# Dilated attention for a prompt: three dilation patterns in sequence, or two pairs of blocks each in turn

## The chip, the core and the metric

The kernel runs on one core of one Trainium2 chip. The metric is the device time of one execution in microseconds (us). The core has TensorE (PE in the profile, with its weight loads as PEld), VectorE (DVE), ScalarE (ACT), GpSimd (POOL) and SyncE (SP, which issues most DMAs here). The profile also gives the clock that TensorE was granted in each stretch, as a share of full speed.

## The reference

One layer of a hybrid decoder trunk, for a prompt of 2048 tokens and a small group of samples. The prompt's attention is the part that matters here:

```python
DIL_PATTERNS = ((128, 1), (512, 4), (2048, 16))     # window, dilation; 8 heads of 64 dims
def _dilated_branch_prompt(q, k, v, dilation, slopes):
    # the tokens of one residue mod `dilation`, in blocks of 128 queries;
    # a block of queries sees its own block of keys and the one before it
    scores = jnp.einsum('bnqchd,bnkchd->bnchqk', qb, kb).astype(jnp.float32) * (HEAD_DIM ** -0.5)
    scores = jnp.where(valid, scores + bias, NEG)
    m = jnp.max(scores, axis=-1, keepdims=True)
    p = jnp.exp(scores - m)
    l = jnp.sum(p, axis=-1, keepdims=True)
    out = jnp.einsum('bnchqk,bnkchd->bnqchd', (p / l).astype(v.dtype), vb)
    lse = m + jnp.log(l)
# the three patterns' outputs are merged with weights softmax(lse)
```

Before it stand the norm and the projection to q, k, v and a pooling input; behind it the output projection and a feed-forward network with a causal convolution, which is most of the time.

## The kernel before

The program has three parts: projections, attention, and output projection with the feed-forward network. Scores and projections use the type float32r (values split into a high and a low part), transposes and products with values use float32.

Attention works on *items*. Each of the 8 heads has three patterns p = 0, 1, 2 (dilation 1, 4, 16), each pattern 16 blocks of 128 queries, and an item is a pair of blocks: 8 items a pattern, 24 a head, 192 in all. A block with a predecessor has 256 keys, one without has 128. Of pattern 0 that is one block in 16 with 128 keys, of pattern 1 four, of pattern 2 all 16: its score matmuls are half as wide, and it has half the transposes and value products. An item is numbered by its place in the list `items` (item 48 is the first of head 2).

An item passes three steps. `scores` (L288, L289): for each block two matmuls (high and low keys) into the PSUM tile `Sp`, of which there are 4; DVE adds the bias table, takes the minimum (L291) and ACT the exponential into `Pt` (L293; 3 buffers). `turn`, two items later: PE transposes (L301), DVE or ACT copies to `PTs` (L304, L306). `values`, three items later: PE multiplies with the values `V` into `Op` (L322; the profile shows two instructions for each such matmul), ACT copies to `O` (L326), and a finished half of a pattern is stored to DRAM (`store_o`).

For patterns 1 and 2 the queries of a head are first copied by POOL into the order of the blocks (`spread_q`, L242: 1024 columns, two buffers). Queries and keys of the next head come in six DMAs of 512 KB (`load_head`, tile `QK`, two buffers) in the third item of a head. Values are held for two heads at a time, 1 MB per pattern in three buffers (`next_v`); those of pattern 2 are loaded in an even head, behind that head's `QK` loads, those of patterns 0 and 1 in the odd head before. All of these go through SP's queue in one order, with the stores between them.

The kernel's framework schedules instructions at build time: each engine gets a fixed list, which is not the order of the source. By its own estimate of when a load lands it lets an engine's later work go ahead of work that would wait. At run time each engine takes its list in order.

The order of the items is this line, and each item calls `advance`:

```python
items = [(h, p, pr) for h in range(H) for p in ((0, 1, 2) if h < H - 1 else (2, 1, 0)) for pr in range(8)]
```

Of the kernel before, what the change touches and what calls it, by code (L numbers as in the profile page):

```python
# [17 lines left out]
P = 128  # L18
# [29 lines left out]
def kernel(ctx, tc, ins, cst, outs):  # L48
# [131 lines left out]
    def load_v(hp, p, t, blocks=slice(0, 16)):  # L180
        vs = v_s[:, hp * P:(hp + 1) * P]
        d = t[:, :, 1:P + 1]
        if p == 0:
            nc.sync.dma_start(d[:, blocks], vs.rearrange("(n i) f -> i n f", i=P)[:, blocks])
        else:
            r, n = DILS[p], S // (P * DILS[p])
            for J in range(n):
                src = vs[J * P * r:(J + 1) * P * r].rearrange("(m c i) f -> i m c f", c=r, i=RUN)
                for i in range(RUN):
                    nc.sync.dma_start(d[i::RUN, r * J:r * (J + 1), :], src[i])  # L190
# [27 lines left out]

    def store_o(p, hp, O, half):
        eng = nc.gpsimd if hp == 3 and p == 0 and half else nc.sync  # L220
        dst = o_s[p * S:(p + 1) * S, hp, :]
        s = slice(8 * half, 8 * half + 8)
        if p == 0:
            eng.dma_start(dst.rearrange("(n i) f -> i n f", i=P)[:, s], O[:, s])
        elif p == 1:
            for J in (2 * half, 2 * half + 1):
                eng.dma_start(dst[J * CH:(J + 1) * CH].rearrange("(i c) f -> i c f", c=4),
                                  O[:, 4 * J:4 * J + 4, :])
        else:
            eng.dma_start(dst.rearrange("(i c) f -> i c f", c=16)[:, s], O[:, s])  # L230

    def spread_q(h, p, half):

        qs = spread[h, p, half] = p2.tile([P, S // 2], F32R, tag="qs", name="qs", bufs=2)
        q, r = heads[h][0], DILS[p]
        if p == 1:
            src = q[:, half * (S // 2):(half + 1) * (S // 2)].rearrange("p (b j c) -> p b c j", b=2, c=r)
            dst = qs.rearrange("p (b c j) -> p b c j", b=2, c=r)
        else:
            src = q.rearrange("p (j c) -> p c j", c=r)[:, half * r // 2:(half + 1) * r // 2]  # L240
            dst = qs.rearrange("p (c j) -> p c j", j=P)
        nc.gpsimd.tensor_copy(dst, src)  # L242
# [8 lines left out]
    def next_v(hp, p):  # L251
        pair_v[hp, p] = value_tile(p2, "V")
        load_v(hp, p, pair_v[hp, p])
# [1016 lines left out]
```

## Time and profile before

| | |
|---|---|
| median of 3 runs | 2542.49 us (2539.44 to 2546.87) |
| the profiled execution | 2538.81 us, its span 2537.0 us |
| mean granted TensorE clock | 0.985 of full speed |
| attention, first score matmul to last value product | 444.8 to 792.9 us of the span |
| busy share of PE, DVE, ACT, POOL | 98%, 68%, 43%, 7% |

Matmuls are pipelined and their ends are modelled, so PE's busy share says little; more is read from how many instructions it gets through in a stretch (the xcount of a row), from the granted clock beside it, and from the waits in brackets in the list of instructions.

### The profile page before, as it was taken

Reading aid. Unit: us, or ns where it says so; the run is one execution under the profiler, and the core shown is the slowest. Engines: PE = TensorE matmul, PEld = TensorE weight load, DVE = VectorE, ACT = ScalarE, POOL = GpSimd, SP = SyncE. Lnnn points to the kernel's source line nnn. Section 1 sums busy time; section 2 is a strip of 40 time slices with the busy share of each in tenths; the row PEclk is TensorE's granted clock in tenths of the full one; section 3 lists DMA queues with packets and bytes.
Section 4 is the critical chain, followed back from the end, with each engine's and each line's share of the span. In section 5 each row is a group of like instructions: output and inputs, shape, how many; then the busy total and the mean of one; then the engine's idle time right before and its main releaser. Section 6 shows DMA issues by size and latency. Waiting matters only on the chain.

```text
span 2537.0 us, 36098 instructions
## 1 busy us (share of the span) xinstructions
PE 2497.4 (98%) x13310; PEld 2126.6 (84%) x13310; DVE 1729.4 (68%) x3819; ACT 1085.1 (43%) x2021; POOL 180.7 (7%) x192
## 2 busy tenths in 40 slices
PE   7999999999998999999999999999999999999999
PEld 5888887899997887888888888888888889999997
DVE  6445445566566775988887788887887666566655
ACT  6333332566564222544443454443443444444442
POOL 1111111222222000000000000000000000000000
PEclk9999999899889999999999999999999999999999
DMA  6343434876655898755558334447443446222321
GB/s 223 102 128 103 129 98 122 197 187 167 143 136 200 286 302 256 238 183 173 182 167 267 100 119 135 145 143 237 145 134 107 125 133 208 87 82 85 93 77 62
DMA packets 412573, 393.60 MB, mean 155 GB/s; under 512 B 16043, under 2 KB 319239, under 8 KB 409708
## 3 DMA queue, kind: packets, MB, share of 16 engines
q1 hardware_dynamic: 412172, 390.48, 50.6%
q8 instruction: 105, 1.72, 0.3%
q0 software_dynamic: 224, 0.80, 0.1%
q14 instruction: 72, 0.59, 0.1%
HBM read 305.70 MB, written 85.52 MB: 154 GB/s over the span
## 4 chain that ended last, share of the span: by engine, by line
PE 94%; DMA 2%; DVE 2%; issue 1%; ACT 0%; POOL 0%; SPq 0%; DVEq 0%; ACTq 0%; POOLq 0%
PE pu L1014 39%; PE pd L1190 19%; PE ps L454 13%; PE po L793 6%; PE Op L322 5%; PE tp L301 3%; PE Sp L288 3%; PE Sp L289 2%; PE tp L122 1%; PE tp L463 1%; PE pd L1184 1%; DVE T L291 0%; PE pp L535 0%; DMA QK<-kT_lo 0%; DMA g_b<-in_g_q_dram 0%
## 5 line engine op out<-in xcount | busy, mean ns | idle before, releaser
L1014 PE MATMUL pu<-h,w 128*128 128x512 f32 (+1 forms) x5232 | 989.0, 349 | 2.2 <-ACT w L112 1.7
L1014 PEld LDWEIGHTS pu<-h,w 128*128 128x128 f32 x5232 | 850.0, 188 | 133.0 <-ACT w L112 2.1
L1190 PE MATMUL pd<-w,act 128*128 128x512 f32 x2112 | 490.2, 392 | 0.0
L1190 PEld LDWEIGHTS pd<-w,act 128*128 128x128 f32 x2112 | 396.7, 188 | 88.0
L112 ACT CAST w<-raw 128x1024 fp32r<-128x1024 f32 (+1 forms) x282 | 286.9, 1026 | 295.4 <-PE pd L1190 187.7
L113 DVE TENSOR_TENSOR w<-raw,w 128x1024 fp32r<-128x1024 f32 (+1 forms) x278 | 329.1, 1187 | 24.3 <-ACT w L112 24.2
L454 PE MATMUL ps<-W_hi,xh 128*128 128x512 f32 x1024 | 332.7, 398 | 1.0 <-ACT xh L112 1.0
L1158 DVE SCALAR_TENSOR_TENSOR cv<-ex,cw,cv 128x512 f32<-128x512 f32 x352 | 262.5, 746 | 29.3 <-ACT cv L1150 26.8
L1148 ACT COPY ex<-pu 128x512 f32<-128x512 f32 (+1 forms) x220 | 110.2, 501 | 341.3 <-PE pu L1014 341.1
L454 PEld LDWEIGHTS ps<-W_hi,xh 128*128 128x128 f32 x1024 | 192.8, 189 | 43.1 <-ACT xh L112 1.5
L291 DVE CUSTOM_DVE_ANT_0 T<-Sp,tab 128x256 f32<-128x256 f32 (+1 forms) x384 | 129.4, 364 | 121.5 <-PE Sp L289 75.9
L293 ACT ACTIVATE Pt<-T,st 128x256 f32<-128x256 f32 (+1 forms) x384 | 162.7, 459 | 97.6 <-DVE st L291 84.1
L454 PE MATMUL ps<-W_lo,xh 128*128 128x512 f32 x512 | 202.8, 396 | 0.0
L1192 DVE TENSOR_TENSOR ya<-ya,pd 128x512 f32<-128x512 f32 x192 | 131.2, 685 | 103.0 <-PE pd L1190 102.4
L95 POOL TENSOR_TENSOR rs<-ms,mhalf 128x8 f32<-128x8 f32 (+3 forms) x68 | 76.4, 1124 | 1584.2 <-DVE stT L1151 1047.7
L322 PE MATMUL Op<-V,PTs 128*128 128x65 f32 x1200 | 174.7, 281 | 0.7 <-DVE PTs L304 0.6
L322 PEld LDWEIGHTS Op<-V,PTs 128*128 128x128 f32 x1200 | 167.2, 207 | 1.7 <-DVE PTs L304 0.8
L1150 ACT ACTIVATE cv<-pu,cw 128x512 f32<-128x512 f32 (+3 forms) x264 | 166.0, 649 | 0.0
L301 PE MATMUL tp<-ident,Pt 128*128 128x128 f32 x600 | 124.4, 294 | 0.1
L112 ACT CAST act<-cv 128x512 fp32r<-128x512 f32 x88 | 54.6, 621 | 159.9 <-DVE cv L1167 153.3
L454 PEld LDWEIGHTS ps<-W_lo,xh 128*128 128x128 f32 x512 | 96.9, 189 | 19.8
L1151 DVE COPY stT<-ex 128x2 f32<-128x2 f32 x176 | 28.9, 164 | 117.7 <-ACT ex L1148 117.5
(225 smaller groups left out, 2759.0 us busy)
## 6 DMA issues: line engine op xcount, KB each, us to landing
raw<-in_w_up_dram SPq DMA_DIRECT2D x176, 512.0 KB
raw<-in_w_down_dram SPq DMA_DIRECT2D x80, 512.0 KB
hn_s<-w SPq DMA_DIRECT2D x16, 1024.0 KB
h<-hn_s SPq DMA_DIRECT2D x32, 512.0 KB
far<-in_cache_k_dram SPq DMA_DIRECT2D x64, 256.0 KB
far<-in_cache_v_dram SPq DMA_DIRECT2D x64, 256.0 KB
om<-o_s SPq DMA_DIRECT2D x16, 792.0 KB
raw<-in_w_in_dram SPq DMA_DIRECT2D x16, 512.0 KB
```

The source lines that it names most:

```text
L112: nc.scalar.copy(hi, src)
L113: (eng or nc.vector).tensor_tensor(out=lo, in0=src, in1=f32(hi), op=ALU.subtract)
L293: nc.scalar.activation(Pt[:, s, :w], T[:, :w], AF.Exp, bias=st[:, i8:i8 + 1], scale=-1.0)
L301: nc.tensor.transpose(tp[:, j, :], Pt[:, s, n * P:(n + 1) * P], ident)
L322: nc.tensor.matmul(Op[:, i4, :], PT[:, j, :], pair_v[hp, p][:, b, v0:v0 + DH + 1], start=n == 0, stop=n == m - 1)
L454: nc.tensor.matmul(ps, xh[:, a, k, :], (W_hi, W_lo)[b][j, k // 2][:, k % 2, :], start=n == 0, stop=n == 3 * KT - 1)
L793: nc.tensor.matmul(ps, lhs, wo[half][k + 4 * (1 - part)][b], start=part == 0 and k == 0 and i == 0, stop=part == 1 and k == 3 and i == 2)
L1014: nc.tensor.matmul(ps[:, :n], w[:, a, k, :], hs[k][:, b, c0:c0 + n], start=i == 0, stop=i == 3 * KT - 1)
L1150: nc.scalar.activation(d, s, AF.Identity, bias=cw[:, 3, ct:ct + 1], scale=cw[:, 2, ct:ct + 1])
L1158: nc.vector.scalar_tensor_tensor(out=d, in0=e[j], scalar=cw[:, j, ct:ct + 1], in1=d, op0=ALU.mult, op1=ALU.add)
L1190: nc.tensor.matmul(ps, act[0][:, a, k, tau * P:(tau + 1) * P], wd[k][:, b, :], start=k == 0 and j == 0, stop=k == n - 1 and j == 2)
L1192: nc.vector.tensor_tensor(out=ysl, in0=ysl, in1=ps, op=ALU.add)
```

## The change

The order of the items becomes one of turns. A turn is two items (four blocks) of one pattern; a head of 1 to 6 takes pattern 0, 2, 1, 0, 2, 1 and so on, four turns each. Head 0 begins with the eight items of pattern 0 as before, head 7 has an order of its own. To go with it, values come in halves of a pattern (8 blocks, six buffers), outputs too, and the copied queries in quarters (512 columns, four buffers, issued six items ahead instead of three). The running minimum `st` and the PSUM tile `Op` are kept per pattern. The first halves of the values of a pair of heads are loaded in the odd head before, all second halves in the even head, behind the loads of `QK`.

```diff
-        t = pool.tile([P, 16, P + 2], F32, tag=tag, name="V", bufs=3 if tag == "V" else 1)
+        t = pool.tile([P, 8 if tag == "V" else 16, P + 2], F32, tag=tag, name="V", bufs=6 if tag == "V" else 1)
...
-    def spread_q(h, p, half):
-
-        qs = spread[h, p, half] = p2.tile([P, S // 2], F32R, tag="qs", name="qs", bufs=2)
+    def spread_q(h, p, k):
+
+        qs = spread[h, p, k] = p2.tile([P, CH], F32R, tag="qs", name="qs", bufs=4)
...
-    def next_v(hp, p):
-        pair_v[hp, p] = value_tile(p2, "V")
-        load_v(hp, p, pair_v[hp, p])
+    def next_v(hp, p, half):
+        t = value_tile(p2, "V")
+        load_v(hp, p, t, 8 * half, 8 * half + 8)
+        for b in range(8):
+            pair_v[hp, p, 8 * half + b] = t[:, b, :]
...
-    items = [(h, p, pr) for h in range(H) for p in ((0, 1, 2) if h < H - 1 else (2, 1, 0)) for pr in range(8)]
+    def turns(seq):
+        at = {}
+        for p in seq:
+            n = at[p] = at.get(p, -1) + 1
+            yield from ((p, 2 * n), (p, 2 * n + 1))
+
+    ORDER = [(0, 0, 0, 0) + (2, 1) * 4] + [(0, 2, 1) * 4] * (H - 2) + [(0, 2, 2, 1, 2, 0, 2, 1, 0, 1, 1, 0)]
+    items = [(h, p, pr) for h in range(H) for p, pr in turns(ORDER[h])]
+    NI = 24
     AHEAD = 8
+    SPREAD = 6
...
-        next_v(0, 1)
-        next_v(0, 2)
+        for half in range(2):
+            for p in (2, 1):
+                next_v(0, p, half)
...
-                h, p, pr = items[i]
-                if (i == AHEAD or h and p == 0 and pr == 3) and h + 1 < H:
+                h, li = divmod(i, NI)
+                if (i == AHEAD or h and li == 4) and h + 1 < H:
                     load_head(h + 1)
-                if h % 2 == 1 and h + 1 < H and p > 0 and pr == 4:
-                    next_v((h + 1) // 2, p - 1)
-                if h % 2 == 0 and h and p == 0 and pr == 4:
-                    next_v(h // 2, 2)
+                for k, p in enumerate((2, 0, 1)):
+                    if h % 2 == 1 and h + 1 < H and li == (14, 17, 21)[k]:
+                        next_v((h + 1) // 2, p, 0)
+                    if h % 2 == 0 and h and li == 4 + k:
+                        next_v(h // 2, p, 1)
```

What the scheduler makes of it shows at the end of head 2. PE before, where `Sp` 5699 to 5809 are items 68 to 73, `qs` marks patterns 1 and 2, and `V_5293` is pattern 2's values: score matmuls of 20 in a row (here the last ten), and then the value products of item 64 and the transposes of item 66.

```order
L289 MATMUL Sp_5745<-QK_4654,qs_5628 128x128
L288 MATMUL Sp_5766<-QK_4654,qs_5628 128x128
L289 MATMUL Sp_5766<-QK_4654,qs_5628 128x128
L288 MATMUL Sp_5789<-QK_5260 128x128
L288 MATMUL Sp_5725<-QK_4654,qs_5628 128x128
L289 MATMUL Sp_5725<-QK_4654,qs_5628 128x128
L288 MATMUL Sp_5809<-QK_5260 128x256
L288 MATMUL Sp_5745<-QK_4654,qs_5628 128x128
L289 MATMUL Sp_5745<-QK_4654,qs_5628 128x128
L289 MATMUL Sp_5789<-QK_5260 128x128
L289 MATMUL Sp_5809<-QK_5260 128x256
L322 MATMUL Op_5695<-V_5293,PTs_5669 128x65 x2
```

PE now at the same place, where `Sp` 5686 to 5814 are items 66 to 71 and `V_5327`, `V_5359`, `V_5387` are the second halves of the values of patterns 2, 0 and 1 (lines have moved: L289 and L290 are the scores, L302 the transposes, L324 the value products).

```order
L290 MATMUL Sp_5686<-QK_4704 128x256
L289 MATMUL Sp_5791<-QK_4704,qs_5640 128x256
L290 MATMUL Sp_5791<-QK_4704,qs_5640 128x256
L289 MATMUL Sp_5708<-QK_4704 128x256
L290 MATMUL Sp_5708<-QK_4704 128x256
L289 MATMUL Sp_5814<-QK_4704,qs_5640 128x256
L290 MATMUL Sp_5814<-QK_4704,qs_5640 128x256
L289 MATMUL Sp_5735<-QK_4704,qs_5585 128x128
L290 MATMUL Sp_5735<-QK_4704,qs_5585 128x128
L324 MATMUL Op_5683<-V_5327,PTs_5658 128x65 x2
L302 MATMUL tp2_5698<-ident_63,Pt_5644 128x128 x4
L324 MATMUL Op_5683<-V_5327,PTs_5680 128x65
```

The run of score matmuls without a transpose or value product is still there, now 19 long, 13 of them 256 wide; before it was 20, of which 2 are 256 wide. What follows it now, up to the next scores of item 72, is this:

```order
L324 MATMUL Op_5633<-V_5359,PTs_5605 128x65 x3
L324 MATMUL Op_5633<-V_5359,PTs_5630 128x65 x4
L324 MATMUL Op_5683<-V_5327,PTs_5680 128x65
L302 MATMUL tp2_5720<-ident_63,Pt_5666 128x128 x4
L324 MATMUL Op_5728<-V_5130,PTs_5703 128x65
L302 MATMUL tp2_5747<-ident_63,Pt_5687 128x128 x4
L289 MATMUL Sp_5765<-QK_4704,qs_5585 128x128
L290 MATMUL Sp_5765<-QK_4704,qs_5585 128x128
L324 MATMUL Op_5728<-V_5387,PTs_5703 128x65
L324 MATMUL Op_5728<-V_5130,PTs_5703 128x65
```

With the rows around them that is 12 transposes, 19 value products (38 instructions in a profile) and two score matmuls. Heads 4 and 6 have such a run at the same place in both kernels, head 0 a shorter one. On SP's queue in head 2, the loads of the next head's `QK` stand ahead of the second halves of the values:

```order
L231 DMA o_s_80<-O_4554 512x1x132 x2
L161 DMA QK_5318<-qT_hi_71 64x2048
L162 DMA QK_5318<-qT_lo_72 64x2048
L165 DMA QK_5318<-kT_hi_73 64x2048
L166 DMA QK_5318<-kT_lo_74 64x2048
L165 DMA QK_5318<-kT_hi_73 64x2048
L166 DMA QK_5318<-kT_lo_74 64x2048
L193 DMA V_5327<-v_s_75 32x8x128 x4
L185 DMA V_5359<-v_s_75 128x8x128
L193 DMA V_5387<-v_s_75 32x4x128 x8
```

Before, the store ahead of them was one DMA (`O_4503`), and behind them stood only the four DMAs of pattern 2's values, of 256 KB each.

## Rows read from the trace of the kernel before

**Rows 1.** The page: busy time by engine, and the clock in 40 slices.
```profile
PE 2497.4 (98%) x13310; PEld 2126.6 (84%) x13310; DVE 1729.4 (68%) x3819; ACT 1085.1 (43%) x2021; POOL 180.7 (7%) x192
...
PEclk9999999899889999999999999999999999999999
```

**Rows 2.** Stretches by head, counting L293's exponentials: length, ACT busy, clock, DMA.
```profile
495.30:532.80 37.50, 20.48 (x48) 1.00 0.72 170
532.80:574.70 41.90, 20.32 (x49) 0.94 0.77 194
...
746.20:790.90 44.70, 20.01 (x48) 0.80 0.24 73
```

**Rows 3.** Stretches with all engines: PE, PEld, DVE, ACT, POOL, clock, DMA, GB/s.
```profile
484.30:491.20 6.90, 5.81 (x29) 5.47 (x29) 2.53 (x15) 2.43 (x7) 0.00 (x0) 0.51 0.53 109
569.70:579.90 10.20, 10.20 (x52) 10.04 (x52) 4.02 (x19) 4.66 (x13) 4.30 (x3) 0.50 0.52 116
651.60:665.20 13.60, 13.37 (x65) 13.22 (x66) 4.19 (x21) 4.91 (x13) 4.26 (x3) 0.50 0.39 85
736.90:764.20 27.30, 27.23 (x133) 26.31 (x134) 13.99 (x64) 13.70 (x40) 7.24 (x6) 0.50 0.21 68
579.90:590.10 10.20, 10.20 (x93) 9.92 (x92) 7.06 (x29) 7.15 (x17) 0.20 (x1) 1.00 0.99 205
487.70:491.10 3.40, 3.40 (x20) 3.40 (x18) 1.45 (x7) 2.03 (x6) 0.00 (x0) 0.50 0.12 29
491.20:494.60 3.40, 3.40 (x30) 3.20 (x30) 1.38 (x5) 1.82 (x5) 2.35 (x3) 1.00 0.51 130
```

**Rows 4.** PE's instructions at the end of head 2, with waits.
```profile
564.71 0.33 PE L288 MATMUL Sp<-QK,qs 128*128 128x128 f32 x1 [0.20 <-DVE st L291]
...
565.87 0.33 PE L288 MATMUL Sp<-QK,qs 128*128 128x128 f32 x1 [0.28 <-DVE st L291]
...
566.82 0.33 PE L288 MATMUL Sp<-QK 128*128 128x128 f32 x1 [0.17 <-DVE st L291]
...
567.98 0.39 PE L288 MATMUL Sp<-QK 128*128 128x256 f32 x1 [0.50 <-DVE st L291]
...
568.75 0.55 PE L322 MATMUL Op<-V,PTs 128*128 128x65 f32 x4
```

**Rows 5.** PE's waits, 455 to 790 us: total, times, longest.
```profile
PE Sp L288 <- DVE st L291: 6.9, 21, 0.7
```

**Rows 6.** DVE by form, 447 to 792 us: busy, mean ns, idle before.
```profile
L291 DVE CUSTOM_DVE_ANT_0 T<-Sp,tab 128x256 f32<-128x256 f32 x216 | 85.2, 422 | 70.4 <-PE Sp L289 44.8 <-ACT O L326 13.0 <-PE tp L301 7.5
...
L291 DVE CUSTOM_DVE_ANT_0 T<-Sp,tab 128x128 f32<-128x128 f32 x168 | 45.4, 290 | 51.1 <-PE Sp L289 31.2 <-PE tp L301 12.1 <-ACT Pt L293 5.8
L291 DVE DVE_READ_ACCUMULATOR2_ANT st<- 128x1 f32 x384 | 31.9, 83 | 0.0
L304 DVE COPY PTs<-tp 128x256 f32<-128x256 f32 x56 | 23.6, 421 | 11.6 <-PE tp L301 11.4
```

**Rows 7.** PE's instructions at the end of head 0, behind its run.
```profile
486.71 1.05 PE L322 MATMUL Op<-V,PTs 128*128 128x65 f32 x4
487.56 0.63 PE L301 MATMUL tp<-ident,Pt 128*128 128x128 f32 x2
...
491.31 0.31 PE L288 MATMUL Sp<-QK,qs 128*128 128x128 f32 x1
```

**Rows 8.** SP's queue in heads 1 and 2: start, time, what it issues.
```profile
526.81 10.27 SPq L190 DMA_DIRECT2D V<-v_s  x16
...
540.24 0.53 SPq L161 DMA_DIRECT2D QK<-qT_hi  x1
```

**Rows 9.** Stretches of DMA in heads 1 and 2, columns as in rows 3.
```profile
541.00:561.00 20.00, 19.97 (x173) 19.31 (x172) 13.78 (x58) 13.43 (x33) 4.39 (x5) 1.00 1.04 230
526.80:537.10 10.30, 10.30 (x89) 10.06 (x89) 6.71 (x37) 7.29 (x22) 6.75 (x7) 1.00 0.43 115
```

**Rows 10.** POOL's instructions as attention begins.
```profile
458.38 2.02 POOL L242 CAST qs<-QK 128x1024 fp32r<-128x1024 f32 x1 [1.20 <-DMA QK<-qT_lo]
```

More of the change, by code (lines that the diff above doesn't have):

```diff
@@ L178, in value_tile, with load_v @@
         return t
-    def load_v(hp, p, t, blocks=slice(0, 16)):
+    def load_v(hp, p, t, lo, hi):
         vs = v_s[:, hp * P:(hp + 1) * P]
@@ L313, in values @@
         st, Pt, blocks = res
-        if h2 == 0 and pr == 0 and h + p:
-            pair_o[p] = p2.tile([P, 16, OW], F32, tag="O", name="O", bufs=3)
-        O = pair_o[p]
+        half, pr4 = divmod(pr, 4)
+        if h2 == 0 and pr4 == 0 and (p, half) not in pair_o:
+            pair_o[p, half] = p2.tile([P, 8, OW], F32, tag="O", name="O", bufs=6)
+        O = pair_o[p, half]
         if pr % 2 == 0:
-            state["Op"] = psum.tile([P, 4, DH + 1], F32, tag="tp", name="Op", bufs=4)
-        Op = state["Op"]
+            state["Op", p] = psum.tile([P, 4, DH + 1], F32, tag="tp", name="Op", bufs=4)
+        Op = state["Op", p]
         v0 = h2 * (DH + 1)
         for j, (s, i4, n, b, m) in enumerate(blocks):
-            nc.tensor.matmul(Op[:, i4, :], PT[:, j, :], pair_v[hp, p][:, b, v0:v0 + DH + 1],
+            nc.tensor.matmul(Op[:, i4, :], PT[:, j, :], pair_v[hp, p, b][:, v0:v0 + DH + 1],
                              start=n == 0, stop=n == m - 1)
@@ L325, in values, with spread_next @@
         if pr % 2:
-            nc.scalar.copy(O[:, 2 * pr - 2:2 * pr + 2, o0:o0 + DH + 1], Op)
-        if pr % 4 == 3:
-            nc.gpsimd.tensor_copy(O[:, 2 * pr - 6:2 * pr + 2, o0 + DH + 1], st)
-        if h2 == 1 and pr % 4 == 3:
-            store_o(p, hp, O, pr // 4)
-    items = [(h, p, pr) for h in range(H) for p in ((0, 1, 2) if h < H - 1 else (2, 1, 0)) for pr in range(8)]
+            nc.scalar.copy(O[:, 2 * pr4 - 2:2 * pr4 + 2, o0:o0 + DH + 1], Op)
+        if pr4 == 3:
+            nc.gpsimd.tensor_copy(O[:, :, o0 + DH + 1], st)
+            if h2 == 1:
+                store_o(p, hp, O, half)
+                del pair_o[p, half]
+    def turns(seq):
[6 more added lines that the diff above has]
+    NI = 24
     AHEAD = 8
+    SPREAD = 6
     attn, PTs = {}, {}
-    SPREAD = 3
+    def spread_next(i):
+        if i < len(items):
+            h, p, pr = items[i]
+            if p and pr % 2 == 0:
+                spread_q(h, p, pr // 2)
     def advance(i):
-        if i + SPREAD < len(items):
-            h, p, pr = items[i + SPREAD]
-            if p and pr % 4 == 0 and i + SPREAD >= 2 * AHEAD:
-                spread_q(h, p, pr // 4)
+        if i >= AHEAD:
+            spread_next(i + SPREAD)
         if i < len(items):
@@ L710 @@
                     param_turn(j - 1)
[L711 to L716 removed]
+                if h == 6 and li % 3 == 0:
+                    k = li // 3
+                    raw = p2.tile([P, CH], F32, tag="row", name="rawo", bufs=2)
+                    nc.sync.dma_start(raw, wov[:, k, 0:CH])
+                    split(wo0[k][:, 0, 0:CH], wo0[k][:, 1, 0:CH], raw)
+                if (h, li) == (7, 0):
                     mBs[0] = load_pool(0)
```

63 lines of the change are left out of this document (29 added, 34 removed).

## The prediction

> **What bounds the kernel now.** The page comes first [rows 1]: PE is busy for 98% of the span, and the granted clock, near full for the whole program, dips in the middle, where attention lies. So I leave the rest of the program alone and cut attention into heads with the view of stretches, using the 48 exponentials of a head as a ruler [rows 2]. Head 1 takes 37.5 us at a clock of 1.00; head 2 takes 41.9 us at 0.94 and head 7, the last, 44.7 us at 0.80. The work of each is the same, so the difference is what there is to win.
>
> The same view in shorter stretches finds where it goes [rows 3]: in four places the clock stands at 0.50, the lower of its two levels (1.2 against 2.4 GHz), for 6.9, 10.2, 13.6 and 27.3 us, 58.0 in sum. PE gets through 52 matmuls in 10.2 us there and through 93 in the 10.2 us that follow at full clock, so a half-clock stretch loses 1 - 52/93 = 0.44 of itself: 58.0 x 0.44 = 25.5 us. What PE did before the clock fell is read from its instructions [rows 4]: at 564.7 to 568.0 us it ran nothing but score matmuls, nearly all of pattern 2 and 128 wide, and stood still four times for DVE's minimum over them, 0.17 to 0.50 us each, since only four `Sp` tiles are there to run ahead with. A microsecond after the first value product, at 569.7, the clock was halved. The list of waits has all of these in one row: 6.9 us in 21 waits [rows 5]. That list of PE's waits in attention names no DMA.
>
> So attention is bound by PE, with two losses on top: 25.5 us of clock and about 6.9 us of waits for DVE. The wait is small; what it costs is the clock after it.
>
> **The change part by part.** *What it leaves.* All matmuls, exponentials, minima and copies are the same in number and shape; only their order differs. At the full-clock rate this is worth nothing either way: PE has no time to give back.
>
> *The run of scores.* The order shows that the scheduler still lets scores run ahead at the ends of heads 2, 4 and 6 and in head 0. So the waits stay, and their size changes with the width. DVE takes 290 + 83 = 373 ns for a narrow block and 422 + 83 = 505 ns for a wide one [rows 6]; PE gets through a matmul in 10.2 us / 93 = 0.11 us [rows 3]. From item 64's first block to item 68's second, DVE has eight wide blocks and two copies for transposes, 8 x 0.505 + 2 x 0.421 = 4.9 us; PE has 26 score matmuls and four transposes, 30 x 0.11 = 3.3 us. If DVE never pauses, PE waits for the difference, 1.6 us a run: the lower end. If none of the eight minima is hidden, it waits 8 x 0.505 = 4.0 us: the upper. In rows 4 four waits of 0.17, 0.20, 0.28 and 0.50 us make 1.15, on average 0.29, a little less than one narrow minimum; so I take four waits of a wide one, 4 x 0.505 = 2.0 us a run, near the lower end. Four runs make 8.0 us against 4 x 1.15 = 4.6 now: +3.4 us, with ends of 6.4 - 4.6 = +1.8 and 16.0 - 4.6 = +11.4. A gain is excluded as long as the run stands in the order, because wider blocks only lengthen DVE's part.
>
> *The clock.* A run with waits is there as before, so I expect the clock to fall at the same four places. What differs is what comes next. In heads 2 and 4 the clock came back after 10.2 and 13.6 us; in the last after 27.3, because at half clock PE went from pattern 2 of head 6 straight into pattern 2 of head 7, 16 narrow items, and came back only when the wide scores of pattern 1 were reached. Head 0's run was followed by transposes and value products alone, 486.7 to 491.3 [rows 7], and there the clock was back at 491.2, 4.5 us after the first of them and 6.9 us after its fall [rows 3]. In the changed order each run is followed by such work alone: 12 transposes and 38 value instructions with two narrow scores among them. So I take head 0's 6.9 us for each place: 4 x 6.9 x 0.44 = 12.1 us. The ends are no fall at all, 0, and the second longest of now, 13.6 us each, 23.9 us. The saving is 25.5 - 12.1 = 13.4 us.
>
> A rule speaks against this part. The Trainium skill ("TensorE: Matmul & The Clock Gate", section "A second HAM failure mode: psum-queue depth-cycling") says that short idles of PE while it cycles through PSUM buffers make its clock swing between the two levels. Rows 4 agree, with waits of at most 0.50 us before a fall; as the four `Sp` tiles stay, by this rule the swings stay too, which is the first rival below. The same page (section "Part 4: PE-mode transpose") says that transposes do not count as busy work for the clock as other matmuls do. By that, a catch-up with many transposes would hold the clock down; in rows 7 and 3 it rose after 8 transposes in 4.6 us, so the trace does not show it.
>
> *The loads.* The same bytes go through SP's queue; value loads are 24 DMAs per pair of heads for patterns 1 and 2 instead of 20. What moves is the deadline. In an even head 3.1 MB of `QK` were issued from 540.2, 7.4 us after the head's first exponential at 532.8 [rows 8, 2], and now three half tiles, 1.57 MB, stand behind them instead of 1.05 MB. At 230 GB/s [rows 9] `QK` is through 21.1 us into the head, the second halves of patterns 2, 0 and 1 at 23.4, 25.7 and 28.0 us, or 30.3 if the eight small DMAs of pattern 1 go at the 115 GB/s that the 16 like them made [rows 8, 9]. The first product that needs pattern 2's second half stands behind item 71's scores: 17 items at 37.5/24 = 1.56 us and six items' scores ahead of time, 6 x 4 x 0.11 = 2.6, so 29.2 us; pattern 1's half is needed behind the 38 value instructions, 38 x 0.11 = 4.2 us later, at 33.4. All come in time, the last with 3 to 5 us to spare. Cost 0; if that cover is gone PE waits in its list, with all transposes and scores behind it (second rival).
>
> *The copies.* POOL's 32 copies of 2.02 us become 64 of half the columns, issued six items, 6 x 1.56 = 9.4 us, ahead; POOL is 7% busy [rows 1], and nothing else on it is due. Cost 0; if a first copy is not covered, PE waits for the copy itself, half of 2.02 us [rows 10]: 1.0 us is the upper end, and nothing here can gain. SP's stores now interleave with the loads as the order shows; no term.
>
> *The sum.* -13.4 + 3.4 = -10.0 us on the profiled execution's 2538.8: 2528.8 us. The median of the runs is 3.7 us above that execution; on its scale the forecast is 2542.5 - 10.0 = 2532 us, which I give.
>
> **The rivals.** *The falls last as long as now.* The run's waits halve the clock, and the catch-up behind it goes on at half speed as in heads 2 and 4. For it: in heads 2 and 4 a catch-up that also began with value products needed 10 to 14 us. Against it: head 0, and no second stretch of pattern 2. At 13.6 us a place: 25.5 - 23.9 = 1.6 saved, 3.4 spent, 2544 us.
>
> *Values come late (slower).* The place is the first product with `V_5387` or `V_5359` behind the run in heads 2, 4, 6; it decides once the queue is over 3 us later than worked out, as when a store ahead of `QK` holds SP. For it: two stores stand ahead of `QK` in the order now, one before, and the second halves are the last of 4.7 MB. At 5 us a head, 15 us, with falls as long as now (+1.8): 2542.5 + 16.8 = 2559 us. Against it: no wait for a DMA in the list of PE's waits, though the queue carries nearly as much.
>
> *No fall at all.* The run of rows 4, which ended in a fall, was narrow but for 2 of its 20 scores; one with 13 wide of 19 has not been seen to end in one: -25.5 + 3.4 = -22.1, 2520 us. Against it: as many waits, and longer.
>
> *The change does not do what it says.* Partly so: the patterns take turns in the source, but the scheduler bunches them. That is in the forecast.
>
> **How the numbers follow.** Forecast 0.50, falls as long 0.20, no fall 0.17, late values 0.13. Within 0.3% means 2534.9 to 2550.1 us, about what a measurement of this kernel can tell from no change. Of the forecast's 0.50, 0.38 lies below and 0.12 in it; no fall is faster; of the second case 0.17 is in it and 0.03 above; of the last 0.02 in it and the rest above. That gives faster 0.55, same 0.31, slower 0.14. The range runs from a little under the no-fall case to the end of the long-falls case: 2514 to 2549 us, with most of the late-values case and the luckiest of no fall left out.
>
> **What would show it.** Right: half-clock stretches behind the ends of heads 2, 4, 6 and in head 0 of some 7 us each, none near 27; waits of L289 for DVE of 6 to 11 us in sum; heads 3 and 5 near 38 to 39 us. Wrong: a wait of L324 for a V load, half-clock stretches of 10 us or more at each place, or no half clock at all; a wait for POOL's `qs`.

## The result, and the profile after

The changed kernel takes 2560.68 us (median of 12 runs, 2549.75 to 2561.97) against 2542.36 us before (12 runs): a ratio of the means of 1.0062, interval 1.0049 to 1.0075. It is slower by 0.6% where 0.4% faster was forecast, and 2560.7 us lies above the stated range. The profiled execution took 2556.11 us, 17.3 us more than that of before, and its rows answer to those shown ahead.

The clock in 40 slices, from the page of the changed kernel. PE is busy for 98% of the span, as in [rows 1]; the clock has two slices at 8 where it had three, so this view does not show the loss.

```profile
PEclk9999999998899999999999999999999999999999
```

Stretches by head with ACT's exponentials as the ruler (L294 now): length, ACT busy, clock, DMA. First heads 1 and 2, then two pairs of heads, 2 with 3 and 4 with 5, then heads 6 and 7.

```profile
495.60:533.10 37.50, 20.20 (x48) 1.00 0.66 161
533.10:584.30 51.20, 20.66 (x49) 0.80 0.63 143
533.10:625.20 92.10, 41.32 (x98) 0.87 0.59 140
625.20:717.60 92.40, 41.18 (x97) 0.87 0.59 139
717.60:765.00 47.40, 20.76 (x50) 0.89 0.78 201
765.00:808.70 43.70, 19.95 (x48) 0.92 0.26 81
```

The same pairs of heads in the kernel before:

```profile
532.80:615.70 82.90, 40.73 (x97) 0.94 0.74 182
615.70:701.30 85.60, 40.75 (x97) 0.92 0.65 151
```

Head 1 is the same to a tenth. Head 2 takes 51.2 us where it took 41.9 [rows 2], the two pairs 9.2 and 6.8 us more. Where the clock stood at 0.50 is in the next view (columns as in [rows 3]; the last row is a full-clock stretch behind the first):

```profile
563.90:587.80 23.90, 23.60 (x115) 23.07 (x115) 7.01 (x27) 7.96 (x20) 4.63 (x5) 0.50 0.37 80
656.10:680.00 23.90, 23.60 (x113) 23.07 (x113) 6.64 (x28) 7.38 (x19) 4.77 (x6) 0.50 0.34 73
748.30:758.50 10.20, 9.56 (x47) 9.27 (x46) 2.26 (x10) 3.19 (x9) 0.20 (x1) 0.50 0.80 276
782.40:789.20 6.80, 6.31 (x29) 5.94 (x30) 2.83 (x14) 3.00 (x8) 1.12 (x2) 0.50 0.00 1
...
588.00:598.20 10.20, 10.20 (x91) 9.89 (x89) 5.89 (x31) 6.16 (x17) 2.18 (x2) 1.00 0.62 128
```

The falls are where they were forecast at heads 2, 4 and 6; head 0 has none, head 7 has one. But they last 23.9, 23.9 and 10.2 us, not 6.9, and make 64.8 us in sum against 58.0 before. A stretch loses 1 - (115/23.9)/(91/10.2) = 0.46 of itself: 29.8 us, some 4 us more than the 25.5 of before. The other executions, which were not traced, say much the same: the mean granted clock of the twelve lies between 0.979 and 0.984, that of the kernel before between 0.978 and 0.985.

PE's instructions at the end of head 2, the run and what follows it:

```profile
559.15 0.31 PE L289 MATMUL Sp<-QK,qs 128*128 128x128 f32 x1 [0.26 <-DVE st L292]
...
560.55 0.33 PE L289 MATMUL Sp<-QK,qs 128*128 128x128 f32 x1 [0.63 <-DVE st L292]
...
562.13 0.36 PE L289 MATMUL Sp<-QK,qs 128*128 128x256 f32 x1 [0.73 <-DVE st L292]
...
563.52 0.38 PE L289 MATMUL Sp<-QK,qs 128*128 128x256 f32 x1 [0.64 <-DVE st L292]
...
564.09 1.06 PE L324 MATMUL Op<-V,PTs 128*128 128x65 f32 x4
564.95 1.06 PE L302 MATMUL tp<-ident,Pt 128*128 128x128 f32 x4
565.80 3.94 PE L324 MATMUL Op<-V,PTs 128*128 128x65 f32 x18
569.54 1.06 PE L302 MATMUL tp<-ident,Pt 128*128 128x128 f32 x4
...
571.88 3.19 PE L324 MATMUL Op<-V,PTs 128*128 128x65 f32 x14
```

Four waits make 2.26 us in this run. Then come 38 value instructions with 12 transposes and two scores among them, all at half clock. The third fall begins in the run itself (748.3), and PE does the same things behind it:

```profile
752.17 3.94 PE L324 MATMUL Op<-V,PTs 128*128 128x65 f32 x18
755.90 1.06 PE L302 MATMUL tp<-ident,Pt 128*128 128x128 f32 x4
756.76 0.52 PE L324 MATMUL Op<-V,PTs 128*128 128x65 f32 x2
757.08 1.06 PE L302 MATMUL tp<-ident,Pt 128*128 128x128 f32 x4
757.79 0.45 PE L289 MATMUL Sp<-QK,qs 128*128 128x128 f32 x1
```

The clock is back at 758.5, behind eight transposes, two value instructions and two scores; in head 2 the same piece (569.5 to 571.9) did not bring it back. So the same work behind a fall took 23.9 us of half clock in heads 2 and 4 and 10.2 us in head 6.

PE's waits from 460 to 806 us (total, times, longest), which answers to [rows 5]; no load of `V` and no `qs` stands in that list:

```profile
PE Sp L289 <- DVE st L292: 12.9, 28, 0.9
```

So attention is 16.0 us longer, from its first score to its last value product (447.2 to 811.3). Some 4 us of that are clock. PE's waits from there to there, of all kinds, are 16.2 us against 8.7: 7.5 us more, 6.0 of them in the row above. The rest, 4 to 5 us, lies between the matmuls at full clock: in the two stretches from 587.8 to 656.1 and 680.0 to 748.3 PE needed 0.120 us a matmul beside its waits, in the same places before (579.9 to 651.6 and 665.3 to 736.9) 0.118, and attention has some 2300 such matmuls. What makes them slower is not shown. Before attention the profiled execution lost 2.4 us, most of it in one wait for a load of a state (1.7 us); behind it, it won 1.1.

### The profile page after: what moved, and what is told of

The parts are those of the page before. It is cut to its first block, busy times and chain, and to the rows that moved or that the text cites. A ratio compares the mean times of both kernels' runs of the same rounds, so it can differ in the third digit from the quotient of the medians.

```text
span 2554.3 us, 36221 instructions
## 1 busy us (share of the span) xinstructions
PE 2506.3 (98%) x13310; PEld 2132.3 (83%) x13310; DVE 1730.4 (68%) x3819; ACT 1087.0 (43%) x2021; POOL 186.9 (7%) x246
## 4 chain that ended last, share of the span: by engine, by line
PE 93%; DMA 2%; DVE 2%; SPq 1%; issue 1%; ACT 1%; POOL 0%; DVEq 0%; ACTq 0%; POOLq 0%
PE pu L1036 38%; PE pd L1212 19%; PE ps L470 13%; PE po L815 6%; PE Op L324 5%; PE tp L302 2%; PE Sp L289 2%; PE Sp L290 2%; DMA QK<-kT_lo 1%; PE tp L122 1%; PE tp L479 1%; PE pd L1206 1%; DVE T L292 1%; PE pp L551 0%; SPq L193 0%
## 5 line engine op out<-in xcount | busy, mean ns | idle before, releaser
L294 ACT ACTIVATE Pt<-T,st 128x256 f32<-128x256 f32 (+1 forms) x384 | 163.6, 459 | 87.0 <-DVE st L292 74.7
L324 PE MATMUL Op<-V,PTs 128*128 128x65 f32 x1200 | 178.3, 286 | 0.9 <-DVE PTs L305 0.6
L324 PEld LDWEIGHTS Op<-V,PTs 128*128 128x128 f32 x1200 | 169.7, 211 | 2.0 <-DVE PTs L305 1.2
L112 ACT CAST act<-cv 128x512 fp32r<-128x512 f32 x88 | 54.6, 620 | 172.9 <-DVE cv L1189 166.6
L302 PE MATMUL tp<-ident,Pt 128*128 128x128 f32 x600 | 118.8, 297 | 0.7 <-ACT Pt L294 0.7
```

Of the source, the lines that this page charges most:

```text
L112: nc.scalar.copy(hi, src)
L294: nc.scalar.activation(Pt[:, s, :w], T[:, :w], AF.Exp, bias=st[:, i8:i8 + 1], scale=-1.0)
L302: nc.tensor.transpose(tp[:, j, :], Pt[:, s, n * P:(n + 1) * P], ident)
L324: nc.tensor.matmul(Op[:, i4, :], PT[:, j, :], pair_v[hp, p, b][:, v0:v0 + DH + 1], start=n == 0, stop=n == m - 1)
```

## The experiments

### The runs taken out by later loads of QK

Each ratio is to runs of the kernel before that were taken beside it; their medians lie between 2544.7 and 2546.2 us, so ratios compare better than times.

In the first, the next head's `QK` goes behind the second halves of the values and a parameter row, so that the scheduler no longer thinks these late and makes no run.

```diff
-                if (i == AHEAD or h and li == 4) and h + 1 < H:
+                if (i == AHEAD or h and li == (4 if h % 2 else 9)) and h + 1 < H:
```

> The changed kernel, with one edit: in heads 2, 4 and 6 the next head's QK is loaded in the tenth item of the head instead of the fifth, behind the second halves of the values and behind the parameter row of the ninth item. In the instruction order the runs of 16 to 19 score matmuls at the ends of heads 2, 4 and 6 are gone; patterns still take turns. Theory A (the time is lost in the run of scores and in the half-clock stretch behind it): no half clock at the ends of heads 2, 4, 6, heads 2 to 6 near 37.5 to 39 us each instead of 51.2, 40.9, 52.0, 40.4, 47.4 (44 us over five clean heads), so some 40 us less than the changed kernel: 2512 to 2527 us, faster than the kernel before. Theory B (taking turns costs time wherever it is done: the spacing of matmuls at full clock was 0.120 us against 0.118, and values or queries come late): still above 2545 us. If the late QK makes PE wait at the start of heads 3, 5, 7, a wait of the first scores for a DMA shows it.

Measured: 2533.3 us, 0.9966 of before (0.9946 to 0.9985). Pairs of heads 2 and 3, 4 and 5, 6 and 7:

```profile
537.40:618.00 80.60, 41.17 (x97) 1.00 0.67 160
618.00:699.40 81.40, 41.14 (x97) 1.00 0.67 160
699.40:781.00 81.60, 40.53 (x97) 1.00 0.58 158
```

From 512.6 us on, attention has no half clock, and PE waits 3.6 us for DVE there. Theory A holds: some 24 us go with the runs alone (1.0062 to 0.9966). In all but one of its twelve executions the mean clock lies above the changed kernel's 0.979 to 0.984 (0.982 to 0.995). The pair that took 92.1 us takes 80.6; the 11.5 us are 23.9 x 0.46 = 11.0 of clock and the rest waits. The time still misses the 2512 to 2527 expected. The ruler was wrong: two heads at full clock take 80 us, not twice head 1's 37.5; and a fall of 17.1 us (495.5 to 512.6) came where no run stands, behind 16 value instructions in a row and waits of at most 0.46 us. So a run is one place for a fall and not the only one.

The second makes the same edit in the kernel before, where these loads stand in a head's fourth item (not the third, as said ahead).

```diff
-                if (i == AHEAD or h and p == 0 and pr == 3) and h + 1 < H:
+                if (i == AHEAD or h and 8 * p + pr == (3 if h % 2 else 9)) and h + 1 < H:
```

> The kernel before, with the same edit: in heads 2, 4 and 6 the next head's QK is loaded in the tenth item instead of the fourth, behind pattern 2's values and a parameter row. The runs of 20 scores at the ends of heads 2, 4 and 6 are gone from the order; patterns in sequence as before. Theory A: no half clock there; heads 2 to 6 took 25.8 us more than five clean heads of 37.5 us and head 7 some 7 more, of which most goes: 2510 to 2520 us. Theory B says nothing of it, but if the clock falls in pattern 2 for its narrow matmuls and not for the run (theory C), half-clock stretches stay at the ends of heads 2, 4 and 6 and the time stays at 2535 to 2545 us.

Measured: 2534.1 us, 0.9956 (0.9941 to 0.9971). The pairs 2 and 3, 4 and 5, and below them the ends of head 0 and of head 6, where head 7 begins (the seam):

```profile
537.30:616.40 79.10, 40.91 (x98) 1.00 0.72 165
616.40:696.20 79.80, 40.82 (x97) 1.00 0.71 162
...
484.60:505.10 20.50, 19.16 (x88) 18.33 (x89) 6.82 (x32) 7.74 (x20) 6.22 (x4) 0.50 0.79 167
...
737.20:764.50 27.30, 26.46 (x124) 24.66 (x124) 13.24 (x64) 14.22 (x38) 5.84 (x6) 0.50 0.28 88
```

Heads 2 to 5 are clean, as theory A says, but the time misses its 2510 to 2520 us: the seam keeps its 27.3 us, where ten scores stand in a row instead of 20, and head 0 has 20.5 us where the kernel before had 6.9 [rows 3]. Nothing was changed in head 0. PE's list is the same there, and so are the four waits in its run (0.20, 0.28, 0.38 and 0.71 us): the same work gave 6.9 us of half clock in one execution and 20.5 in another. At full clock a pair in turns takes 1.5 to 1.6 us more than one in sequence (80.6 and 81.4 against 79.1 and 79.8), some 6 us if four pairs do: so much of theory B is true. Most of it is waits: in heads 4 and 5 PE waits 2.1 us in turns (1.3 for DVE's minimum, 0.6 for its copies, 0.2 for ACT) and 0.7 in sequence. With the runs out of both, turns win nothing: 0.9966 against 0.9956.

The third keeps halves and quarters, and takes the turns away.

```diff
-    ORDER = [(0, 0, 0, 0) + (2, 1) * 4] + [(0, 2, 1) * 4] * (H - 2) + [(0, 2, 2, 1, 2, 0, 2, 1, 0, 1, 1, 0)]
+    ORDER = [(0,) * 4 + (1,) * 4 + (2,) * 4] * (H - 1) + [(2,) * 4 + (1,) * 4 + (0,) * 4]
```

> The changed kernel with its halves of values and outputs and quarters of queries, but the patterns of a head in sequence 0, 1, 2 as before (2, 1, 0 in head 7). The order has a run of 16 score matmuls, 14 of them wide, at item 60 of head 2 and in the same place of heads 4 and 6, each followed by 11 value products. Theory A: falls at these places and near item 18 of head 0, with waits of wide minima; between the two kernels, 2545 to 2560 us. Theory B (turns cost, halves do not): as the kernel before, 2538 to 2545 us.

Measured: 2597.6 us, 1.0197 (1.0172 to 1.0223), outside what either theory expected. PE's waits for loads in attention:

```profile
PE Op L324 <- DMA V<-v_s: 20.2, 3, 7.6
```

The values came late: in sequence, pattern 0's second half is wanted by a head's fifth item, with `QK` and a half of pattern 2 ahead of it in the queue. In heads 2, 4 and 6 PE waits at the 33rd of a head's 150 value instructions, the first to read that half. This is what the second rival feared, in another order: three waits of 5.9 to 7.6 us and half clock of 54.6, 30.7 and 27.3 us about them. So it is no test of halves without turns; one stands further down.

The fourth moves `QK` by three items only.

```diff
-                if (i == AHEAD or h and li == 4) and h + 1 < H:
+                if (i == AHEAD or h and li == (4 if h % 2 else 7)) and h + 1 < H:
```

> The changed kernel with QK loaded in the eighth item of heads 2, 4 and 6, behind the second halves of the values but ahead of the parameter row. In the order a run of 18 scores (10 wide) stands at items 69 to 74 in heads 2 and 4, none in head 6, and what follows it mixes transposes, scores and value products, with no seven value products in a row. Theory A: falls in heads 2 and 4 only; since the work behind the run is mixed they end after 7 to 14 us, not 24: 2528 to 2542 us. If the length of a fall does not hang on what follows the run, 24 us each again: 2545 to 2552 us. Theory B: as the changed kernel, 2550 or more.

Measured: 2543.3 us, 0.9988 (0.9962 to 1.0014); its twelve runs lie between 2526.7 and 2563.4, and the profiled one is among the shortest. There a run of 18 scores with waits of 0.85 and 0.98 us cost 6.8 us of half clock in head 2 and nothing in head 4, where the same run with the same waits stands. The second of these waits in each head, and the clock behind it:

```profile
568.58 0.58 PE L289 MATMUL Sp<-QK,qs 128*128 128x256 f32 x1 [0.98 <-DVE st L292]
...
651.18 0.39 PE L289 MATMUL Sp<-QK,qs 128*128 128x256 f32 x1 [0.98 <-DVE st L292]
```

```profile
567.80:574.60 6.80, 6.02 (x30) 5.87 (x31) 1.98 (x8) 1.32 (x4) 4.50 (x6) 0.50 0.58 129
640.00:780.00 140.00, 135.08 (x1125) 127.80 (x1125) 91.93 (x397) 91.20 (x231) 35.07 (x59) 1.00 0.58 150
```

A run with waits makes a fall likely, not sure. That a fall behind mixed work is short, as expected, is not shown: over the twelve executions the mean clock goes from 0.994, the profiled one's, down to 0.976, lower than in any of the changed kernel's.

### What makes a fall last

Value products have 65 columns, scores and transposes 128 or 256. In the next kernel they are 128 wide; the added columns are thrown away.

```diff
-            state["Op", p] = psum.tile([P, 4, DH + 1], F32, tag="tp", name="Op", bufs=4)
+            state["Op", p] = psum.tile([P, 4, P], F32, tag="tp", name="Op", bufs=4)
...
-        v0 = h2 * (DH + 1)
+        v0 = 2 * h2
...
-            nc.tensor.matmul(Op[:, i4, :], PT[:, j, :], pair_v[hp, p, b][:, v0:v0 + DH + 1],
+            nc.tensor.matmul(Op[:, i4, :], PT[:, j, :], pair_v[hp, p, b][:, v0:v0 + P],
...
+            nc.scalar.copy(O[:, 2 * pr4 - 2:2 * pr4 + 2, o0:o0 + DH + 1], Op[:, :, 63 * h2:63 * h2 + DH + 1])
```

> The changed kernel with value products 128 columns wide instead of 65 (the other head's columns beside this head's, thrown away when Op is copied), 1200 instructions as before. The order keeps runs of 18 and 19 scores, 13 of them wide, at the ends of heads 4 and 6; at the end of head 2 the run is cut in two, 11 and 13. What follows a run is again transposes and value products. Theory M (the long falls of heads 2 and 4 last because what follows the run is mostly 65-wide value products): behind the runs in heads 4 and 6 half clock lasts under 14 us or does not come. Rival N (the length has to do with the waits inside the run, or with chance): about 24 us in head 4 again. A transpose, 128 wide, is spaced 0.116 us at full clock against 0.103 for a value instruction, so the width may cost up to 1200 x 0.013 = 16 us at full clock; the time itself, 2545 to 2575 us, tells little, the lengths of the half-clock stretches tell it.

Measured: 2555.7 us, 1.0043 (1.0028 to 1.0058). The half-clock stretches of heads 4 and 6, behind runs of 18 and 19 scores, and then heads 3 and 4 together:

```profile
656.90:660.30 3.40, 3.12 (x14) 3.13 (x15) 0.43 (x4) 0.38 (x1) 0.20 (x1) 0.50 0.02 5
749.10:752.50 3.40, 3.40 (x18) 3.40 (x18) 0.30 (x2) 1.32 (x3) 0.00 (x0) 0.50 0.01 2
580.30:672.50 92.20, 87.11 (x667) 78.25 (x667) 53.64 (x235) 53.90 (x132) 24.45 (x43) 0.98 0.59 141
```

The falls come as before but last 3.4 us instead of 23.9 and 10.2, and the mean clock of the four executions is 0.993 to 0.995 (0.979 to 0.984 without the wide products). What is won is paid for at full clock: two heads take 92.2 us with only 3.4 us at half clock. So the wide products are set only where a fall lay.

```diff
...
+        li = items.index(it) % NI
+        wide = h in (2, 4, 6) and li >= 14 or h in (3, 5, 7) and li < 6
+        v0, n0, nc_ = (2 * h2, 63 * h2, P) if wide else (h2 * (DH + 1), 0, DH + 1)
```

> The changed kernel with its loads and runs as they are, and value products 128 columns wide only where its long half-clock stretches lay: from the fifteenth item of heads 2, 4 and 6 to the sixth of the next head. The order keeps the runs of 19, 19 and 16 scores. Some 170 value instructions are wide, which costs at most 170 x 0.013 = 2 us at full clock. Theory M (narrow value products behind a run hold the clock at half): falls at the ends of heads 2 and 4 of 3.4 to 7 us instead of 23.9, 2 x 17 to 20 us x 0.44 = 15 to 18 us less than the changed kernel: 2542 to 2548 us, level with the kernel before. Rival N (the wide products of all heads were needed, or the runs of the wholly wide kernel differed): falls of 14 us or more, 2552 us and more.

Measured: 2550.1 us, 1.0015 (1.0004 to 1.0026), so 0.5% less than the changed kernel's 1.0062. The falls behind the runs of heads 2, 4 and 6:

```profile
569.20:576.00 6.80, 5.44 (x24) 4.88 (x24) 1.42 (x8) 0.90 (x2) 0.32 (x2) 0.50 0.75 240
657.90:668.10 10.20, 9.57 (x46) 9.38 (x45) 1.75 (x9) 2.74 (x7) 0.20 (x1) 0.50 0.03 7
746.70:756.90 10.20, 9.48 (x43) 9.22 (x44) 1.66 (x8) 2.81 (x7) 0.20 (x1) 0.50 0.37 110
```

With the same runs of 19, 19 and 16 scores and the same four waits each, 23.9, 23.9 and 10.2 us became 6.8, 10.2 and 10.2: so the first two falls are below N's 14 us, the first alone is as short as theory M hoped, and the third did not change. The mean clock of the twelve executions, 0.985 to 0.991, lies above all of the changed kernel's, so the gain is not one execution's luck. Not all of the work behind the runs was wide: of the 38 value instructions 14 in a row, those of a head's thirteenth and fourteenth items, kept their 65 columns. This execution also fell for 13.7 us at the start of head 1, where the profile of the changed kernel had not.

The same in the kernel before, its runs of 16 and 20 scores untouched:

```diff
...
+        wide = h % 2 == 0 and li >= 16 or h in (1, 3, 5) and li < 4 or h == 7 and li < 12
```

> The kernel before with its loads, and with its runs of 16 and 20 scores where they were, and value products 128 columns wide in pattern 2 of heads 0, 2, 4 and 6, the first four items of heads 1, 3 and 5 and the first twelve of head 7: some 260 instructions, at most 260 x 0.013 = 3.4 us at full clock. Theory M (narrow value products make a fall last): the stretches of 6.9, 10.2, 13.6 and 27.3 us shorten to 3.4 to 7 us each, 58 - 20 = 38 us x 0.44 = 16 us less, 2.5 to 3.4 us more: 2528 to 2532 us. Rival N (the mix of the turned order mattered, not the width): stretches of 10 us and more at heads 4 and 6 to 7, 2538 us and more.

Measured: 2541.3 us, 0.9980 (0.9969 to 0.9991). Its falls, one for one those of [rows 3], and PE behind the run of head 2:

```profile
487.20:494.00 6.80, 6.09 (x29) 5.90 (x30) 1.95 (x10) 2.45 (x8) 0.00 (x0) 0.50 0.54 113
572.50:575.90 3.40, 3.29 (x15) 3.30 (x16) 0.38 (x3) 0.33 (x2) 0.00 (x0) 0.50 0.02 5
654.40:661.20 6.80, 6.43 (x31) 5.79 (x30) 2.76 (x15) 1.91 (x6) 1.11 (x2) 0.50 0.01 4
739.70:743.10 3.40, 3.20 (x15) 3.21 (x16) 1.98 (x7) 0.09 (x1) 0.00 (x0) 0.51 0.35 102
```

```profile
574.05 1.05 PE L324 MATMUL Op<-V,PTs 128*128 128x128 f32 x4
574.90 0.63 PE L301 MATMUL tp<-ident,Pt 128*128 128x128 f32 x2
575.33 0.89 PE L324 MATMUL Op<-V,PTs 128*128 128x128 f32 x4
```

And PE's waits for the copies of the transposes:

```profile
PE Op L324 <- DVE PTs L304: 3.1, 4, 1.2
```

6.9, 10.2, 13.6 and 27.3 us became 6.8, 3.4, 6.8 and 3.4. The transposes are the same in both; only the width of the value products differs. The mean clock of the eleven executions is 0.989 to 0.993, that of the kernel before beside them 0.978 to 0.984, with no overlap: so theory M holds in sequence too, and by more than one execution. The time fell less than the 13 us expected: 37.6 us of half clock x 0.44 = 16.5 us went, and some 5 came out. The waits for `PTs` are one part of the price; how the rest splits was not traced.

### Halves without turns, and the seams

Halves and quarters in sequence, both halves of a pattern loaded together where before the whole was, `QK` in the tenth item of even heads (the lines that replace the loads in turns):

```diff
...
+                for half in range(2):
+                    if h % 2 == 1 and h + 1 < H and li in (12, 20):
+                        next_v((h + 1) // 2, li // 20, half)
+                    if h % 2 == 0 and h and li == 4:
+                        next_v(h // 2, 2, half)
```

> The changed kernel's halves and quarters without the turns and without the runs: patterns of a head in sequence 0, 1, 2 (2, 1, 0 in head 7), both halves of a pattern's values loaded where the kernel before loads the whole, QK in the tenth item of heads 2, 4 and 6. The order has no run over 10 anywhere. If halves and quarters cost nothing, about the time of the kernel before with late QK, 2534 us, or some 10 less because the run in head 0 is gone too: 2520 to 2536 us. If halves cost time by themselves (more DMAs, more copies on POOL, Op and st per pattern): 2540 or more. If turns cost nothing it is level with the changed kernel with late QK, 2533 us.

Measured: 2531.8 us, 0.9949 (0.9937 to 0.9961). Heads 2 and 3 take 79.1 us, 4 and 5 80.2, like the kernel before with late `QK`: halves and quarters are free, and what a pair costs more in turns comes of the order of the items.

The next two work on the kernel before with late `QK`: head 7 in another order (a load at its first item moves along), and then pattern 2's first values over ACT's queue as well.

```diff
-    items = [(h, p, pr) for h in range(H) for p in ((0, 1, 2) if h < H - 1 else (2, 1, 0)) for pr in range(8)]
+    items = [(h, p, pr) for h in range(H) for p in ((0, 1, 2) if h < H - 1 else (1, 2, 0)) for pr in range(8)]
```

> The kernel before with late QK, and head 7 in the order 1, 2, 0 instead of 2, 1, 0, so that pattern 2 of head 6 is not followed by pattern 2 of head 7. Late QK alone still had a half-clock stretch of 27.3 us there (737.2 to 764.5). If that stretch came of 32 narrow items in a row: it goes or is under 11 us, 7 to 12 us less than late QK alone, 2522 to 2528 us. If it is the work of splitting the next weights in head 6 that slows DVE: it stays, 2530 to 2537 us.

Measured: 2528.8 us, 0.9939 (0.9927 to 0.9951). The fall at the seam is 10.2 us instead of 27.3, in line with the expectation that it lasted through the second stretch of pattern 2. Head 0, unchanged again, has 20.5 us (490.7 to 511.2).

```diff
-        next_v(0, 2)
+        next_v(0, 2, nc.scalar)
```

> As the last one, and pattern 2's first values go over ACT's DMA queue instead of SP's, which takes the run of 16 scores in head 0 out of the order. No run over 11 is left in attention. Theory A: no half clock in attention behind its first items (6.8 us there), 0.44 x 20.5 = 9 us less than the last one: 2513 to 2520 us, the fastest of all. If the falls come in any narrow stretch, run or not: half clock still in head 0 or 7, 2522 us or more.

Measured: 2526.4 us, 0.9928 (0.9916 to 0.9941), faster than both kernels. The two falls that are left past attention's first items:

```profile
465.30:479.00 13.70, 13.39 (x62) 13.00 (x63) 5.36 (x25) 5.62 (x14) 2.27 (x3) 0.50 0.73 178
...
738.40:745.20 6.80, 6.67 (x29) 5.83 (x30) 3.45 (x15) 3.06 (x9) 1.96 (x2) 0.50 0.25 77
```

The fall of head 0 has moved from its end to its beginning, behind four waits for DVE of 1.6 us in sum. No run over 11 scores is left, and yet half clock stands in heads 0 and 7 and the time lies above theory A's 2513 to 2520 us: that is what was expected if falls need no run.

Wide value products at the seam of heads 6 and 7, and then with head 7's other order and at the end of head 0 too, both on the halves in sequence:

```diff
...
+        wide = h == 6 and li >= 20 or h == 7 and li < 12
```

> The halves in sequence without runs (2531.8 us, with half clock from 736.5 to 760.4 at the seam of heads 6 and 7), and value products 128 wide from item 21 of head 6 to item 12 of head 7. Theory M: the stretch there shortens from 23.9 to 3.4 to 10 us, 6 to 9 us less: 2523 to 2527 us. Rival: the seam's fall lasts because 16 narrow items follow, whose scores and transposes are few and whose DVE work is late; then it stays over 14 us and 2529 to 2533 us.

```diff
...
+        wide = h == 6 and li >= 20 or h == 7 and li < 8 or h == 0 and li >= 20 or h == 1 and li < 4
```

> The halves in sequence without runs, head 7 in the order 1, 2, 0, and wide value products at two places: the last items of head 0 with the first of head 1, the last of head 6 with the first of head 7. Theory M: half clock at these places 3.4 us at most or none, the fastest kernel: 2518 to 2525 us. If each fall moves to another place once one is removed: above 2526 us.

Measured: 2528.6 us, 0.9930 (0.9917 to 0.9943), the seam's 23.9 us down to 6.8; and 2526.7 us, 0.9924 (0.9910 to 0.9938), with 6.8 and 3.4 us of half clock left past attention's first items. Theory M was right on the fall of the first, whose time lies 1.6 us above the expected end; the second is level with the kernel above, not the fastest by itself as hoped, and its 6.8 us and 2526.7 us are nearer to what was expected if falls move to other places.

Last, the turns without runs, with wide products at the seam of heads 0 and 1, and then at every seam. In the second of these the fifth item of a head is wide and shares its output tile with the sixth, whose narrow columns are copied for both. In odd heads these are the wrong columns for the fifth item, so the kernel's output is not the layer's; the work is the same, and only its times and stretches are used.

```diff
...
+        wide = h == 0 and li >= 16 or h == 1 and li < 6
```

> The changed kernel with late QK (2533 us, with half clock from 495.5 to 512.6) and wide value products in the last items of head 0 and the first of head 1. Theory M: that stretch is gone or under 7 us; the kernel with turns then takes 2520 to 2528 us, and a pair of heads in turns 80.5 to 81.5 us against 79 to 80 in sequence, so that turns by themselves cost some 5 us. If turns by themselves are free it is level with the best kernel in sequence.

```diff
...
+        wide = li >= 20 or li < 5
```

> The changed kernel with late QK (no runs in heads 2, 4 and 6) and value products 128 wide in the last four and the first five items of every head. Some 420 instructions are wide, at most 420 x 0.013 = 5.5 us at full clock. If value products at the seams are what makes the turned kernels fall without a run: half clock in attention behind the first items under 10 us in sum, and times that lie closer together than the 18 to 29 us of the turned kernels with late QK: 2524 to 2532 us. If falls there come of the waits for DVE alone: 20 us of half clock or more, and a spread as before.

Measured: 2532.2 us, 0.9942 (0.9922 to 0.9963), and 2532.3 us, 0.9954 (0.9940 to 0.9968). The first misses the 2520 to 2528 us of theory M: there the seam of heads 0 and 1 is clean, but 20.5 us of half clock stand at 465.1 and 13.7 at the seam of heads 4 and 5 (666.5), where eight value instructions were followed by scores with waits of 0.18 and 0.47 us. In the second:

```profile
466.70:483.80 17.10, 17.10 (x84) 16.65 (x83) 7.43 (x38) 7.77 (x22) 3.55 (x5) 0.50 0.65 159
483.80:790.00 306.20, 297.73 (x2421) 276.32 (x2420) 198.95 (x865) 198.41 (x494) 84.17 (x140) 1.00 0.63 155
```

No seam falls in this execution, and the six runs lie within 9 us of each other, where the twelve of the first and of the fourth kernel spread over 29 and 37 us: that speaks for a part of the value products at the seams, without proving it. The fall in head 0 stays, against the under 10 us expected, and the wide products' price takes up what is won. Turns reached 2532 us, the sequence 2526; the intervals of their best, 0.9922 to 0.9963 and 0.9910 to 0.9938, overlap a little.

## Why the prediction was wrong

The step that failed is "So I take head 0's 6.9 us for each place". It was read from one stretch in which PE did 8 transposes beside some 16 value instructions, and carried over to one with 12 beside 38, on the ground that both hold transposes and value products alone. The falls measured 23.9, 23.9 and 10.2 us behind the runs, and 6.8 in head 7. Instead of 12.1 us the half clock cost 29.8: the term was -13.4 us and came out at +4.

Two things were wrong with the step. The work behind a fall matters: with most of the value products 128 wide the falls behind the runs were 6.8, 10.2 and 10.2 us, and in the order of before 3.4, 6.8 and 3.4 instead of 10.2, 13.6 and 27.3, with a higher mean clock in every execution. So rows with more than twice as many narrow value products were not like head 0's. And head 0's 6.9 us was no fixed length: the same instructions behind the same waits took 20.5 us in the profiles of two later kernels (the second experiment, and the one with head 7's other order). The profile that the forecast was read from was a good one, with a mean clock of 0.985 where the kernel before has 0.978 to 0.985. Why the same work keeps half clock for 6.9 us or 20.5, 10.2 or 23.9, is open; no run here decides it.

The places were right for heads 2, 4 and 6. That the clock falls behind the runs held, and without the runs these falls go (the first experiment, and the second but for head 6). Head 0's did not come in this execution, and one came in head 7, whose new order had waits of up to 0.94 us.

The waits were sized rightly where they were forecast: 2.26 us in the run of head 2 against 2.0, and 7.9 us in the four runs against 8.0. (Before, the four made 5.5 us and not 4.6, since the forecast let head 2's 1.15 us stand for all.) But in sum they are 12.9 us, 6.0 more than before instead of 3.4, over the 6 to 11 expected: head 7, where none were forecast, has 2.5 us of them against 0.5, and single waits stand elsewhere.

"At the full-clock rate this is worth nothing either way" was a second error, of 4 to 5 us: 0.120 us a matmul beside the waits against 0.118. It is not the turns alone that cost this, for without runs a pair of heads in turns takes 1.2 to 1.5 us more than the halves in sequence (80.6 and 81.4 us against 79.1 and 80.2), and most of that is waits; the rest was not traced further.

Loads and copies were right at nothing: no wait for `V` or `qs`. How much of the margin of 3 to 5 us was left no trace tells; the third experiment shows what a late half costs, at another place. Of the rivals, "falls as long as now" was nearest in kind, and 17 us short, in part because it took 13.6 us as the longest that a fall could be, though one of 27.3 stood in [rows 3]. No fall at all is refuted, and late values were not the cause here.

The sum that came out is 4 (clock) + 7.5 (all waits) + 4 to 5 (matmuls at full clock) = some 16 us in attention, against 16.0 measured.

Of the two rules weighed, the one on short idles ("TensorE: Matmul & The Clock Gate" of the Trainium skill, section "A second HAM failure mode: psum-queue depth-cycling") agrees for the most part: falls follow waits of 0.2 to 0.9 us, but one run with waits of 0.85 and 0.98 us had none behind it (fourth experiment). The one on transposes (section "Part 4: PE-mode transpose") would have the transposes behind a run hold the clock down. Here the clock came back behind eight of them in head 6 and stayed down behind the same eight in heads 2 and 4, which decides nothing; but widening the value products alone, with the transposes untouched, cut the falls.

## What to carry to other kernels

The cost of a short wait of PE can lie in what comes behind it: here waits of 2.3 us were followed by 23.9 us of half clock. Do not take a fall's length from one other fall: the same work gave 6.9 and 20.5 us in two executions. Read several executions, or give the term a range that reaches beyond the longest fall seen. When a scheduler bunches work, look for the load that it believes late and move that: one line did more here (0.9956 in sequence, 0.9966 in turns) than the whole new order. And take the clean time of a unit from a stretch as long as the pattern that repeats (here two heads, some 80 us), not from its best part.

## What the runs showed of the hardware

Half clock lasted for 23.9 us while PE was busy nearly all the time (23.60 us of it), in a stretch where more than half of the instructions were 65-column value products; with the value products wide, wholly or in part, the falls behind the runs of heads 2, 4 and 6 were 3.4 to 10.2 us instead of 10.2 to 27.3.

The same instructions behind the same waits are not always followed by the same clock: 6.9 us of half clock in one execution and 20.5 in another at the end of head 0, 6.8 us in head 2 and none in head 4 of one execution behind waits of 0.85 and 0.98 us. With it, one kernel took from 2526.7 to 2563.4 us, at a mean clock of 0.994 to 0.976 (fourth experiment).
